# A two-layer decoder step on one core: small norm steps moved to GpSimd, one head's state made later, more room for prefetched caches

## The chip, the cores and the metric

The kernel runs on one NeuronCore of a Trainium2 chip. The metric is the device time of one execution in microseconds (us), less is better. The engines are named as the profile names them: PE (TensorE matmul), PEld (its weight load), DVE (VectorE), ACT (ScalarE), POOL (GpSimd) and SP (SyncE, which issues nearly all DMAs). SBUF is the on-chip memory, PSUM the memory that PE writes.

## The reference, cut to what matters

One inference step of two layers, for a prompt of 256 tokens and 8 samples of one token each, which share all weights. D is 1024. Every layer adds three things to x: a mixer, a cross attention to a memory of 256 rows, and a conv FFN, each on rmsnorm(x). Layer 0 mixes by retention, layer 1 by a gated linear recurrence (LRU).

```python
def rmsnorm(x, g):
    return x * lax.rsqrt(jnp.mean(x * x, axis=-1, keepdims=True) + EPS) * g

def retention_mixer(h, s0, offset, w_in, w_out):
    q, k, v, g = jnp.split(h @ w_in, [nqk, 2 * nqk, 2 * nqk + nv], axis=-1)   # 4 heads
    q, k = rotary(q), rotary(k) * RET_DK ** -0.5
    o, s = retention_scan(q, k, v, s0)          # s: new state, 256 x 512 a head
    o = o * lax.rsqrt(jnp.mean(o * o, axis=-1, keepdims=True) + EPS)          # per head
    return (silu(g) * o) @ w_out, s

def rglru_mixer(...):          # two projections, a conv of width 4, two gates, a scan, an output projection
def cross_attn(h, mk, mv, w_q, w_o):   # softmax(q mk') mv, per head; the samples have caches of their own
def conv_ffn(h, buf, w_up, ...):       # gelu(conv(u)) * g, then w_down
```

All arithmetic is float32. The outputs are y, the new retention, LRU and conv states, and the memory's keys and values.

## The kernel before, in words

**Tiling.** Activations lie with features on the 128 partitions and 264 columns (256 prompt tokens, 8 samples). Each weight matrix comes as chunks of 128x1024 float32 (512 KB), streamed by SP into 6 buffers `wraw`. A chunk is split into a rounded high part `wh` (ACT, line 328, at times DVE, line 460) and the rest `wl` (DVE, line 288). The activations are split into A (or B) in the same way, and each product is three matmuls: wh by high, wh by low, wl by high (`mm3`). Small products (attention in the retention part, sums by a matrix of ones, head states, the LRU's gates) are plain float32 matmuls instead.

**Order of the work.** `run` goes through a list of units (weight chunks with their matmuls) and of plain calls. Between matmuls, a scheduler that runs when the program is built lets other work in: generators (tasks) that issue a few instructions and yield. It decides by a model of each engine's clock (`Clock.op` with a cost per instruction) and by table `POLICY`. What it has decided is fixed: every engine runs its own list in order, and waits by semaphores. So a matmul that is placed too early for its input makes PE wait, and all matmuls behind it.

**Stages.** Retention (all four heads, with the memory's keys and values of layer 0 between), cross attention 0, FFN 0, LRU, cross attention 1, FFN 1, final norm. `enter(nb, ...)` opens a stage: it makes B with `nb` rows of 264 columns, an arena `ar` of what is left of SBUF for temporaries and prefetched tensors, and for `nb` under 24 a second arena of FR = 3072 words. In cross attention that arena (`farena`) holds the split parts of K, q, V and p of `xa_prompt`. `prefetch` loads wanted tensors (sample states, caches) while at most `maxpre` are held and the arena keeps `reserve` words free.

**Norms.** `rsqrt_mean` sums squares over partitions by matmuls with a column of ones (three columns of sums for 264 tokens), makes `a = mean + eps` on DVE, and calls `newton` (line 700): a bit trick for a first guess, then three Newton steps of three small DVE instructions each (128x3 elements). Then PE transposes the result back to rows (`tr`, line 284), ACT copies it to SBUF as `r`. This form is used eight times: for the mixer's norm of x (`g` in `start`), for the memory (`mem_norm(0)`, 128x2 elements), for the heads 0 to 3 (`ret_norm`) and for the norms ahead of both cross attentions (`norm_later`). The norms ahead of FFN and LRU use a wide form.

**A head's new prompt state.** At the end of `ret_attn(h)`, kd (decayed keys, 512 words a partition) and vt (values, 1024 words) are multiplied: 4 float32 matmuls of 512 columns in two PSUM banks, each bank copied by ACT to SBUF and stored to `ret_p`.

**LRU and its end.** The output projection waits at two places for the elementwise chain of each half: `lru_half(1)` before the first three chunks, `lru_half(2)` before the next.

Of the kernel before, what the change touches and what calls it, by code (L numbers as in the profile page):

```python
# [19 lines left out]
P = 128  # L20
# [226 lines left out]
class Kern:  # L247
# [452 lines left out]
    def newton(self, a, y, n, root=False):  # L700

        t = self.get(n)
        tv = t.ap[:, :n]
        if root:
            self.act(y, a, AF.Sqrt)
            self.recip(y, y)
        else:
            self.ts(y.bitcast(I32), a.bitcast(I32), 1, None, ALU.logical_shift_right)
            self.ts(y.bitcast(I32), y.bitcast(I32), -1.0, float(0x5F3759DF), MUL, ADD)
        for _ in range(1 if root else 3):  # L710
            self.tt(tv, y, y, MUL)
            self.stt(tv, a, -0.5, tv, MUL, MUL)
            self.stt(y, tv, 1.5, y, ADD, MUL)
        t.free()

    def rsqrt_mean(self, sq, n, cnt, wide=False, tok=None, root=False):

        b = yield from self.wbank()
        if wide:
            ps = self.ps[:, b, :n]  # L720
            self.mm(ps, self.ones, sq, True, True, False)
            a = self.get(n)
            r = self.get(n)
# [12 lines left out]
        self.unbank(b)  # L736
        self.newton(a.ap[:, :w], a.ap[:, 4:4 + w], w, root)
# [20 lines left out]
    def norm_later(self, wide=False):  # L758
# [3 lines left out]
        def g():  # L762
# [3 lines left out]
            self.r = yield from self.rsqrt_mean(self.sq, NT, float(D), wide)  # L766
# [109 lines left out]
    def retention(self):  # L876
        qkv, gs = [], []
        self.hd = [dict(flags=set()) for _ in range(H)]
        for h in range(H):
            hd = self.hd[h]  # L880

            def ev_rot(b, dt, which, hd=hd, h=h):
# [10 lines left out]
                cs = self.cst[:, C_COS:C_COS + 2 * NT].rearrange("p (a b) -> p a b", a=2)  # L893
                sc = self.cst[:, C_SIN:C_SIN + 2 * NT].rearrange("p (a b) -> p a b", a=2)
# [55 lines left out]
    def ret_qk(self, h):  # L950
# [28 lines left out]
        for jt in range(2):  # L979
            self.act(kd.v(2, 256)[:, jt, :], ps[:, jt * 256:(jt + 1) * 256], AF.Identity,  # L980
                     scale=self.cst[:, C_DEC + 2 * h + jt:C_DEC + 2 * h + jt + 1])
# [20 lines left out]
    def ret_attn(self, h):  # L1002
# [14 lines left out]
        mk = self.cst[:, C_MASK + T * h:C_MASK + T * (h + 1)]  # L1017
# [34 lines left out]
        kd = hd["kd"].v(2, 256)  # L1052
        for dt in range(2):
            b = yield from self.wbank()
            for jt in range(2):
                self.mm(self.ps[:, b, :], kd[:, jt, dt * P:(dt + 1) * P], vv[:, jt, :], jt == 0, jt == 1, False)
            yield WAIT
            so = yield from self.wget(512)
            self.cp(so.ap[:, :512], self.ps[:, b, :])
            self.unbank(b)  # L1060
            self.later_free(lambda so=so, dt=dt: self.store(self.o["ret_p"][h, dt], so.ap[:, :512]), so)
        vt.free()
        hd["kd"].free()
        self.unlock("p")
# [93 lines left out]
    def ret_norm(self, h):  # L1158
# [12 lines left out]
        r = yield from self.rsqrt_mean(s[:, 0, :], NT, 512.0)  # L1171
# [585 lines left out]

POLICY = (
# [6 lines left out]
def tile_hybrid_step(ctx: ExitStack, tc: tile.TileContext, ins, outs):  # L1765
# [10 lines left out]
    K.cst = pool.tile([P, NCST], F32, name="cst")  # L1776
    K.par = pool.tile([P, NPRM], F32, name="par")
    K.qk = ctx.enter_context(tc.tile_pool(name="rows", bufs=1, space=bass.MemoryType.DRAM)).tile([H, 2, S, 256], F32, name="qk")
    K.junkt = pool.tile([P, 2, 256], BF16, name="junkt")
# [22 lines left out]
    FR = 3072  # L1802
    ROOM = 29184 + 1024 * (6 - K.NR) - 128 - 128 - S - 2 * 2 * KD * M

    def enter(nb, maxpre, reserve, slots, main):
        def go():
# [3 lines left out]
            fr = FR if nb < 24 else 0  # L1810
            extra = ROOM - 2 * nb * NT - fr
# [3 lines left out]
            if nb == 16:  # L1815
                K.mn = (bt[:, 0, 8:, :M], bt[:, 1, 8:, :M])
            ar = Arena(pb.tile([P, extra], F32, name=f"x{K.uid}"), extra)
            K.ar = ar
            if fr:
                lend(nb == 16)  # L1820
# [7 lines left out]
    def lend(states):  # L1828
# [8 lines left out]
        box.append((fs, ar))  # L1837

    def unlend():
        fs, ar = box.pop()  # L1840
# [3 lines left out]
    def relend():  # L1844
        unlend()
        lend(False)
# [17 lines left out]
    def leave():  # L1864
        K.drain()
        if len(box[-1]) == 2:
            unlend()
# [5 lines left out]
    def start():  # L1873
# [6 lines left out]
        K.load(K.cst[:, :C_MASK], ins["cst"][:, :C_MASK])  # L1880
# [6 lines left out]
        K.load(K.cst[:, C_MASK:], ins["cst"][:, C_MASK:])  # L1887
# [8 lines left out]
        def g():  # L1896
# [11 lines left out]
            cs = K.cst[:, C_COS:C_COS + 3 * NT].rearrange("p (a b) -> p a b", a=3)  # L1908
# [168 lines left out]
```

## Time and profile before

| what | us |
|---|---|
| median of 3 runs | 1028.97 (1027.68 to 1030.23) |
| the profiled execution, its time | 1026.02 |
| the profiled execution, its span | 1024.2 |
| PE busy | 999.7 (98%) |
| DVE busy | 801.8 (78%) |
| ACT busy | 573.1 (56%) |
| POOL busy | 84.1 (8%) |

A span reaches from the first to the last instruction. The granted clock of PE is 0.996 over the span. Rows of groups read: line of the kernel, engine, operation, output <- input, shape, count, busy time, mean length in ns, idle time before. A row of a timeline reads: start, length of the merged instructions from the first start to the last end, engine, line, operation. Instructions of one engine overlap in the record, since the next starts before the one before has drained: the distance from start to start is what an instruction costs its engine. A float32 matmul of the plain form stands as two records for each instruction of the program (the row that says 512 columns x4 is two instructions).

### The profile page before, as it was taken

The page shows a single profiled execution, that of the slowest core. Times are in us where ns is not written, and L with a number is a line of the kernel's source. Part 1 is how long each engine was busy: PE and PEld are TensorE (multiplying, and loading weights), DVE is VectorE, ACT ScalarE, POOL GpSimd, SP SyncE. Part 2 cuts the span into 40 slices and gives each one's busy share as a digit, 9 for nine tenths or more (in the row PEclk, how much of TensorE's full clock was granted, in tenths as well). Part 3 has the DMA queues.
Part 4 walks back from the last instruction along what each step waited for, and adds up shares of the span by engine and source line. Part 5 has one row for each costly group of instructions (what it writes and reads, how often), then busy time and mean ns, then how long its engine had stood idle before and what let it go on. Part 6 is the DMA issues. An engine that isn't in the chain of part 4 may idle for free.

```text
span 1024.2 us, 20780 instructions
## 1 busy us (share of the span) xinstructions
PE 999.7 (98%) x8042; PEld 949.3 (93%) x8042; DVE 801.8 (78%) x1683; ACT 573.1 (56%) x960; POOL 84.1 (8%) x190
## 2 busy tenths in 40 slices
PE   7999999999999999999999999999999999999996
PEld 7989999899998779999999999989867999999996
DVE  6957888687887635899899777989754998999674
ACT  5544445454555545566666554697444676666552
POOL 0000000000000000122231000300000132221000
PEclk9999999999999999999999999999999999999998
DMA  9568787886677976767798887448876678788961
GB/s 369 196 229 298 270 290 244 324 292 219 225 260 258 340 285 233 223 208 231 279 333 301 297 287 249 154 160 302 296 249 208 224 233 272 279 304 270 332 207 75
DMA packets 75619, 263.89 MB, mean 258 GB/s; under 512 B 8640, under 2 KB 9344, under 8 KB 75008
## 3 DMA queue, kind: packets, MB, share of 16 engines
q1 hardware_dynamic: 75088, 261.98, 73.8%
q8 instruction: 63, 1.03, 0.4%
q10 hardware_dynamic: 432, 0.58, 0.2%
q14 instruction: 36, 0.29, 0.1%
HBM read 237.72 MB, written 24.81 MB: 256 GB/s over the span
## 4 chain that ended last, share of the span: by engine, by line
PE 57%; DVE 4%; DMA 3%; ACT 3%; issue 1%; SPq 0%; DVEq 0%; ACTq 0%
PE ps L269 54%; PE ps L274 2%; ACT x L324 1%; DVE wl L288 1%; DVE x L288 1%; DVE x L294 1%; DMA x<-in_cache_v 1%; ACT L324 1%; DMA x<-in_cache_k 1%; DMA kvt<-in_cache_v 1%; PE ps L284 1%; DMA kvt<-in_cache_k 1%; DMA wraw<-in_lru_w_in 0%; DVE x L313 0%; ACT wh L328 0%
## 5 line engine op out<-in xcount | busy, mean ns | idle before, releaser
L269 PE MATMUL ps<-A,wh 128*128 128x264 f32 x2816 | 524.3, 287 | 7.9 <-ACT A L324 6.6
L269 PEld LDWEIGHTS ps<-A,wh 128*128 128x128 f32 x2816 | 437.7, 189 | 16.0 <-issue 7.0
L328 ACT CAST wh<-wraw 128x1024 fp32r<-128x1024 f32 x283 | 296.2, 1050 | 274.1 <-PE ps L269 211.0
L288 DVE TENSOR_TENSOR wl<-wraw,wh 128x1024 fp32r<-128x1024 f32 x296 | 359.2, 1221 | 80.1 <-ACT wh L328 70.8
L269 PE MATMUL ps<-A,wl 128*128 128x264 f32 x1408 | 400.4, 284 | 0.1
L269 PE MATMUL ps<-B,wh 128*128 128x264 f32 (+1 forms) x1664 | 308.6, 286 | 0.9 <-DVE B L288 0.9
L269 PEld LDWEIGHTS ps<-A,wl 128*128 128x128 f32 x1408 | 265.3, 188 | 0.6 <-DVE wl L288 0.5
L269 PEld LDWEIGHTS ps<-B,wh 128*128 128x128 f32 x1664 | 257.0, 188 | 9.0 <-issue 7.5
L269 PE MATMUL ps<-B,wl 128*128 128x264 f32 (+1 forms) x832 | 235.7, 283 | 1.2 <-DVE wl L288 1.2
L269 PEld LDWEIGHTS ps<-B,wl 128*128 128x128 f32 x832 | 156.3, 188 | 1.4 <-DVE wl L288 1.4
L288 DVE TENSOR_TENSOR x<-ps,x 128x264 f32<-128x264 f32 (+2 forms) x248 | 83.4, 364 | 27.8 <-PE ps L269 18.2
L332 POOL COPY x<-x 128x16 f32<-128x16 f32 (+2 forms) x162 | 77.8, 514 | 257.8 <-DVE x L288 199.0
L324 ACT ACTIVATE x<-x 128x264 f32<-128x264 f32 (+4 forms) x166 | 59.6, 389 | 30.5 <-DVE x L294 17.8
L294 DVE SCALAR_TENSOR_TENSOR x<-x,par 128x280 f32<-128x280 f32 (+3 forms) x128 | 61.7, 488 | 2.3
L294 DVE SCALAR_TENSOR_TENSOR junkt<-f,x 128x256 bf16<-128x256 f32 x104 | 37.8, 421 | 20.9 <-DMA f<-in_state_ret 14.8
L294 DVE SCALAR_TENSOR_TENSOR kvt<-x,vst,kvt 128x256 f32<-128x256 f32 x128 | 53.3, 478 | 0.0
L328 ACT CAST B<-x 128x264 fp32r<-128x264 f32 (+2 forms) x84 | 34.7, 418 | 32.6 <-DVE x L288 25.0
L288 DVE TENSOR_TENSOR x<-x 128x264 f32<-128x264 f32 (+6 forms) x106 | 44.8, 435 | 5.7 <-ACT x L324 3.9
L288 DVE TENSOR_TENSOR B<-x,B 128x264 fp32r<-128x264 f32 (+2 forms) x84 | 36.8, 439 | 8.8 <-ACT B L328 8.6
L324 ACT ACTIVATE x<-x,par 128x280 f32<-128x280 f32 (+2 forms) x64 | 38.6, 605 | 5.1 <-DVE x L288 4.7
L269 PE MATMUL ps<-wh,B 128*128 128x512 f32 x128 | 41.4, 397 | 0.0
L328 ACT COPY x<-ps 128x264 f32<-128x264 f32 (+4 forms) x64 | 22.6, 381 | 32.7 <-PE ps L269 20.4
(90 smaller groups left out, 669.9 us busy)
## 6 DMA issues: line engine op xcount, KB each, us to landing
wraw<-in_ffn_w_up SPq DMA_DIRECT2D x96, 512.0 KB, 4.4
wraw<-in_ret_w_in SPq DMA_DIRECT2D x48, 512.0 KB, 4.8
wraw<-in_ffn_w_down SPq DMA_DIRECT2D x48, 512.0 KB, 5.4
kvt<-in_state_ret SPq DMA_DIRECT2D x38, 512.0 KB, 7.0
out_ret_s<-kvt SPq DMA_DIRECT2D x32, 512.0 KB, 6.0
f<-in_state_ret SPq DMA_DIRECT2D x26, 512.0 KB, 5.3
x<-in_cache_v SPq DMA_DIRECT2D x21, 512.0 KB, 7.1
wraw<-in_xa_w_k SPq DMA_DIRECT2D x16, 512.0 KB, 4.4
```

The source lines that it names most:

```text
L269: self.last = self.nc.tensor.matmul(out, lhsT, rhs, start=start, stop=stop)
L274: self.nc.tensor.matmul(out, lhsT, rhs, start=start, stop=stop, tile_position=(0, LO * j))
L284: self.nc.tensor.transpose(out, in_, self.ident[:n, :n])
L288: self.nc.vector.tensor_tensor(out=out, in0=a, in1=b, op=op)
L294: self.nc.vector.scalar_tensor_tensor(out, a, s, b, op0, op1, **kw)
L324: self.nc.scalar.activation(out, in_, func, **kw)
L328: self.nc.scalar.copy(out, in_)
L332: self.nc.gpsimd.tensor_copy(out, in_)
```

## The change

- **Newton steps on POOL.** `newton` has a flag `aside`. With it the three steps run as four `nc.gpsimd` instructions each (12 in all) instead of three on DVE (9 in all); the scheduler's model books 130 ns for each. Set for the norm of x, the memory's norm and the heads 0, 1 and 2. Head 3 and the norms of `norm_later` keep DVE.
- **Head 2's state later.** In `ret_attn(2)` kd and vt are stored to a DRAM tensor `sv` (parked). In the LRU part `state_back(2)` loads them back (768 KB), and `state_gen` makes the state with 8 float32 matmuls of 256 columns. `fill(2, n)` issues n of them at three places: 3 after `lru_half(1)`, 3 after `lru_half(2)`, 2 before cross attention 1. The other heads also use 8 matmuls of 256 columns.
- **Room.** Only the identity and the ones (256 columns of the constants) stay in SBUF for the whole program. The rotary tables, decays and masks (1824 words a partition) lie in a tile `tab` of the first stage. The later stages' arenas grow by that. In the LRU and cross attention 1 stage the second arena shrinks from 3072 to 2048 words, and `maxpre` goes from 3 to 5.

```diff
-    def newton(self, a, y, n, root=False):
+    def newton(self, a, y, n, root=False, aside=False):
...
         for _ in range(1 if root else 3):
+            if aside:
+                for out, ins in ((tv, (y,)), (tv, (tv, a)), (tv, (tv,)), (y, (y, tv))):
+                    self.c.op("pool", 130.0, [out], list(ins))
+                self.nc.gpsimd.tensor_tensor(out=tv, in0=y, in1=y, op=MUL)
+                self.nc.gpsimd.tensor_tensor(out=tv, in0=tv, in1=a, op=MUL)
+                self.nc.gpsimd.tensor_scalar(tv, tv, -0.5, 1.5, MUL, ADD)
+                self.nc.gpsimd.tensor_tensor(out=y, in0=y, in1=tv, op=MUL)
+                continue
             self.tt(tv, y, y, MUL)
...
-    def rsqrt_mean(self, sq, n, cnt, wide=False, tok=None, root=False):
+    def rsqrt_mean(self, sq, n, cnt, wide=False, tok=None, root=False, aside=True):
...
+        if h in PARKED:
+            self.later_free(lambda: self.store(self.sv[h][:, :512], hd["kd"].ap[:, :512]), hd["kd"])
+            self.later_free(lambda: self.store(self.sv[h][:, 512:], vt.ap[:, :1024]), vt)
+        else:
+            for dt in range(2):
+                b = yield from self.wbank()
+                for half in range(2):
+                    for jt in range(2):
+                        self.state_mm(b, hd["kd"], vt, dt, half, jt)
+                yield WAIT
+                yield from self.state_out(b, h, dt)
...
+    def state_mm(self, b, kd, vt, dt, half, jt):
+        c = slice(half * 256, (half + 1) * 256)
+        self.mm(self.ps[:, b, c], kd.v(2, 256)[:, jt, dt * P:(dt + 1) * P], vt.v(2, 512)[:, jt, c], jt == 0, jt == 1, False)
...
+    def fill(self, h, n):
+        def go():
+            for _ in range(n):
+                next(self.fills[h], None)
+        return go
...
-        r = yield from self.rsqrt_mean(s[:, 0, :], NT, 512.0)
+        r = yield from self.rsqrt_mean(s[:, 0, :], NT, 512.0, aside=h < H - 1)
...
+PARKED = (2,)
...
-    K.cst = pool.tile([P, NCST], F32, name="cst")
+    K.cst = pool.tile([P, C_COS], F32, name="cst")
...
+            fr = {16: 3072, 8: 2048, 24: 0}[nb]
+            extra = ROOM - 2 * nb * NT - fr - (TAB if nb == 16 else 0)
...
-    items += [policy(3), enter(8, 3, 4500, (), 6), lambda: K.want_cache(1)] + K.lru()
+    items += [policy(3), enter(8, 5, 4500, (), 6), K.state_back(2), lambda: K.want_cache(1)] + K.lru()
...
-    items += out(w, [K.lru_half(1), pairs(w, (0, 1, 2), (0,)), K.lru_half(2), tune(12, 3500, (0,), 6),
+    items += out(w, [K.lru_half(1), K.fill(2, 3), pairs(w, (0, 1, 2), (0,)), K.lru_half(2), K.fill(2, 3), tune(12, 3500, (0,), 6),
...
-    items += [policy(4), tune(14, 3500, (0,), 4, 1)] + K.xattn(1)
+    items += [policy(4), tune(14, 3500, (0,), 4, 1)] + [K.fill(2, 2)] + K.xattn(1)
```

Since the scheduler's clock sees other costs and sizes, the order of much of the work shifts. Three places matter below. The first is DVE at the norm of head 0's output, in the kernel before. `x_85` is the stage's arena, `junkt` the thrown-away product of the samples' dot products with the old states (`f_89`), `cst` the constants.

```order
L288 TENSOR_TENSOR wl<-wraw,wh 128x1024
L301 TENSOR_SCALAR x_85<-ps 128x3
L299 TENSOR_SCALAR x_85<-x_85 128x3
L301 TENSOR_SCALAR x_85<-x_85 128x3
L288 TENSOR_TENSOR x_85<-x_85 128x3
L294 SCALAR_TENSOR_TENSOR x_85<-x_85 128x3 x2
```

After two more such steps DVE goes on with other work. In the changed kernel DVE has, at the same norm, this (`x_89` is the arena, `f_93` the states):

```order
L301 TENSOR_SCALAR x_89<-ps 128x3
L299 TENSOR_SCALAR x_89<-x_89 128x3
L301 TENSOR_SCALAR x_89<-x_89 128x3
L288 TENSOR_TENSOR wl<-wraw,wh 128x1024
L294 SCALAR_TENSOR_TENSOR junkt,x_89<-f_93,x_89 128x256 x12
L288 TENSOR_TENSOR wl<-wraw,wh 128x1024
L288 TENSOR_TENSOR x_89<-x_89 128x528 x2
```

The Newton steps are gone from DVE, and the instructions that stood behind them follow the three guesses at once. The second place is POOL, which before has nothing between its start and the four `vst` products of the retention part. In the changed kernel its list begins so (one Newton step of the first norm; eight more rows like the last four end that norm):

```order
L714 ISA
L714 TENSOR_TENSOR x_89<-x_89 128x3
L715 TENSOR_TENSOR x_89<-x_89 128x3
L716 TENSOR_SCALAR x_89<-x_89 128x3
L717 TENSOR_TENSOR x_89<-x_89 128x3
```

Five norms put 60 such instructions there, each waiting for the one before. The third place is PE at the two ends of head 2's state. Before, at the end of its attention (`x_85` holds kd and vt):

```order
L269 MATMUL ps<-x_85 128x512 x2
L269 MATMUL ps<-A,wh 128x264 x2
L269 MATMUL ps<-A,wl 128x264
L269 MATMUL ps<-x_85 128x512 x2
L269 MATMUL ps<-A,wh 128x264 x2
```

In the changed kernel these are absent there, and at `lru_half(1)` PE has (`x_6722` is the LRU stage's arena, `B_6721` the projection's input):

```order
L269 MATMUL ps<-A,wl 128x264
L269 MATMUL ps<-x_6722 128x256 x3
L269 MATMUL ps<-B_6721,wh 128x264 x2
L269 MATMUL ps<-B_6721,wl 128x264
L269 MATMUL ps<-B_6721,wh 128x264 x2
```

The same three stand again within the B rows at `lru_half(2)`, and two stand before the first A row of cross attention 1.

## Rows read from the trace of the kernel before

**Rows 1.** The page, part 1: busy time and share of the span by engine.

```profile
PE 999.7 (98%) x8042; PEld 949.3 (93%) x8042; DVE 801.8 (78%) x1683; ACT 573.1 (56%) x960; POOL 84.1 (8%) x190
```

**Rows 2.** Windows: stretch, its length, then busy time (instructions) by engine, clock, DMA.

```profile
20.00:300.00 280.00, 278.83 (x2107) 264.06 (x2105) 222.66 (x597) 137.27 (x221) 2.18 (x5) 1.00 0.76 264
...
440.00:460.00 20.00, 20.00 (x168) 20.00 (x167) 19.28 (x53) 12.74 (x22) 4.09 (x12) 1.00 0.61 201
...
640.00:725.00 85.00, 81.76 (x613) 78.28 (x612) 77.68 (x143) 62.23 (x94) 11.12 (x24) 1.00 0.62 217
725.00:805.00 80.00, 76.04 (x705) 62.12 (x704) 50.58 (x106) 39.20 (x94) 0.00 (x0) 1.00 0.68 233
```

**Rows 3.** Waits of PE in the LRU and cross attention 1: total us, times, longest.

```profile
PE ps L269 <- DVE wl L288: 1.2, 1, 1.2
...
PE ps L269 <- DVE B L288: 0.9, 1, 0.9
...
PE ps L274 <- DMA x<-in_cache_v: 1.6, 1, 1.6
PE ps L274 <- DMA kvt<-in_cache_v: 0.9, 2, 0.5
...
PE ps L274 <- DMA kvt<-in_cache_k: 0.4, 1, 0.4
```

**Rows 4.** Timeline of PE at the end of head 2's attention.

```profile
125.43 1.88 PE L269 MATMUL ps<-x 128*128 128x512 f32 x4
...
129.47 0.28 PE L269 MATMUL ps<-A,wl 128*128 128x264 f32 x1
```

**Rows 5.** Timeline of PE at the first norm: sums, next matmul, transposes.

```profile
20.46 0.72 PE L269 MATMUL ps<-cst,sq 128*128 128x1 f32 x6
21.05 0.49 PE L269 MATMUL ps<-A,wh 128*128 128x264 f32 x2
...
24.42 0.49 PE L284 MATMUL ps<-cst,x 128*128 128x128 f32 x3
```

**Rows 6.** Timeline of DVE at the first norm: mean, first Newton instruction, last two.

```profile
21.23 0.16 DVE L301 TENSOR_SCALAR x<-ps 128x3 f32<-128x3 f32 x1 [2.31 <-PE ps L269]
...
21.83 0.16 DVE L288 TENSOR_TENSOR x<-x 128x3 f32<-128x3 f32 x1
...
23.20 0.36 DVE L294 SCALAR_TENSOR_TENSOR x<-x 128x3 f32<-128x3 f32 x2
```

**Rows 7.** Timelines of POOL and of DVE beside it, in FFN 0.

```profile
427.80 2.33 POOL L332 COPY x<-x 128x2 f32<-128x2 f32 x2 [2.31 <-DVE x L288]
...
427.72 2.35 DVE L288 TENSOR_TENSOR wl<-wraw,wh 128x1024 fp32r<-128x1024 f32 x2
...
447.84 0.34 POOL L332 COPY x<-x 128x2 f32<-128x2 f32 x2 [5.45 <-DVE x L288]
...
447.36 0.83 DVE L288 TENSOR_TENSOR x<-ps,x 128x256 f32<-128x256 f32 x3
```

**Rows 8.** Groups of POOL by shape, whole span.

```profile
L332 POOL COPY x<-x 128x3 f32<-128x3 f32 x8 | 5.4, 672 | 17.6 <-DVE x L288 17.5
...
L1033 POOL TENSOR_TENSOR vst<-x 128x32 f32<-128x32 f32 x3 | 1.0, 327 | 114.2 <-ACT x L328 83.8 <-DVE junkt L294 30.4
```

**Rows 9.** Timeline of DVE behind head 0's norm: one split, dot products with states.

```profile
107.92 1.22 DVE L288 TENSOR_TENSOR wl<-wraw,wh 128x1024 fp32r<-128x1024 f32 x1
109.05 0.42 DVE L294 SCALAR_TENSOR_TENSOR junkt<-f,x 128x256 bf16<-128x256 f32 x1
...
109.40 0.42 DVE L294 SCALAR_TENSOR_TENSOR junkt<-f,x 128x256 bf16<-128x256 f32 x1
```

**Rows 10.** Groups of DVE by shape, whole span.

```profile
L460 DVE CAST wh<-wraw 128x1024 fp32r<-128x1024 f32 x13 | 9.0, 691 | 9.9 <-PE ps L269 9.8
...
L288 DVE TENSOR_TENSOR f<-kvt,f 128x512 fp32r<-128x512 f32 x16 | 10.9, 684 | 0.5 <-ACT f L328 0.5
```

**Rows 11.** Timeline of PE at the sums of head 1's norm.

```profile
140.32 0.80 PE L269 MATMUL ps<-cst,x 128*128 128x1 f32 x6 [0.35 <-DVE x L288]
```

More of the change, by code (lines that the diff above doesn't have):

```diff
@@ L765, in g @@
             yield self.c.written(self.sq)
-            self.r = yield from self.rsqrt_mean(self.sq, NT, float(D), wide)
+            self.r = yield from self.rsqrt_mean(self.sq, NT, float(D), wide, aside=False)
         def go():
@@ L1051, in ret_attn @@
         hd["flags"].add("attn")
-        kd = hd["kd"].v(2, 256)
-        for dt in range(2):
[L1054 to L1061, printed above, removed]
@@ L1062, in ret_attn @@
-        vt.free()
-        hd["kd"].free()
-        self.unlock("p")
+        if h in PARKED:
[9 more added lines that the diff above has]
+                yield from self.state_out(b, h, dt)
+            vt.free()
+            hd["kd"].free()
@@ new lines, in ret_attn, with state_out, state_back, g @@
+        self.unlock("p")
+    def state_mm(self, b, kd, vt, dt, half, jt):
+        c = slice(half * 256, (half + 1) * 256)
+        self.mm(self.ps[:, b, c], kd.v(2, 256)[:, jt, dt * P:(dt + 1) * P], vt.v(2, 512)[:, jt, c], jt == 0, jt == 1, False)
+    def state_out(self, b, h, dt):
+        so = yield from self.wget(512)
+        self.cp(so.ap[:, :512], self.ps[:, b, :])
+        self.unbank(b)
+        self.later_free(lambda: self.store(self.o["ret_p"][h, dt], so.ap[:, :512]), so)
+    def state_back(self, h):
+        def go():
+            def g():
+                b = yield from self.wget(1536)
+                self.load(b.ap[:, :1536], self.sv[h])
+                self.back[h] = b
+            self.add(g(), 0)
+            self.fills[h] = self.state_gen(h)
+        return go
@@ new lines, in state_gen @@
+    def state_gen(self, h):
+        self.until(lambda: h in self.back)
+        buf = self.back[h]
+        kd, vt = (Buf(buf.ap[:, o:], None, 0, 0) for o in (0, 512))
+        for dt in range(2):
+            self.until(lambda: self.aux)
+            b = min(self.aux, key=self.bank_at)
+            self.aux.remove(b)
+            for half in range(2):
+                for jt in range(2):
+                    self.state_mm(b, kd, vt, dt, half, jt)
+                    if half * jt:
+                        self.add(self.state_out(b, h, dt), 1, self.c.t["pe"])
+                        if dt:
+                            buf.free()
+                    yield
@@ L1066, in later_free, with go @@
+    def fill(self, h, n):
+        def go():
+            for _ in range(n):
+                next(self.fills[h], None)
+        return go
     def later_free(self, fn, buf):
@@ L1775, in tile_hybrid_step @@
     K.locks = {}
-    K.cst = pool.tile([P, NCST], F32, name="cst")
+    K.cst = pool.tile([P, C_COS], F32, name="cst")
     K.par = pool.tile([P, NPRM], F32, name="par")
     K.qk = ctx.enter_context(tc.tile_pool(name="rows", bufs=1, space=bass.MemoryType.DRAM)).tile([H, 2, S, 256], F32, name="qk")
+    K.sv = ctx.enter_context(tc.tile_pool(name="parked", bufs=1, space=bass.MemoryType.DRAM)).tile([H, P, 1536], F32, name="sv")
+    K.back, K.fills = {}, {}
     K.junkt = pool.tile([P, 2, 256], BF16, name="junkt")
@@ L1819, in go @@
             if fr:
-                lend(nb == 16)
+                lend(nb == 16, fr)
             tune(maxpre, reserve, slots, main)()
@@ L1826, in enter, with lend @@
         return go
-    def lend(states):
+    def lend(states, FR):
         fs = ExitStack()
@@ L1836, in lend @@
             K.farena = ar
-        box.append((fs, ar))
+        box.append((fs, ar, FR, 0))
     def unlend():
-        fs, ar = box.pop()
+        fs, ar, FR, _ = box.pop()
         K.until(lambda: ar.holes == [(0, FR)])
@@ L1845, in relend @@
         unlend()
-        lend(False)
+        lend(False, 3072)
     def tune(maxpre, reserve, slots, main, p=2):
@@ L1865, in leave @@
         K.drain()
-        if len(box[-1]) == 2:
+        if len(box[-1]) == 4:
             unlend()
@@ L1879, in start @@
         K.fetch()
-        K.load(K.cst[:, :C_MASK], ins["cst"][:, :C_MASK])
+        K.load(K.cst, ins["cst"][:, :C_COS])
+        K.load(K.tab[:, :3 * NT], ins["cst"][:, C_COS:C_MASK])
         def split():
@@ L1886, in start @@
         split()
-        K.load(K.cst[:, C_MASK:], ins["cst"][:, C_MASK:])
+        K.load(K.tab[:, 3 * NT:], ins["cst"][:, C_MASK:])
         K.load(K.par[:, NG:], ins["par"][:, NG:])
```

19 lines of the change are left out of this document (9 added, 10 removed).

## The prediction

> **What bounds the kernel now.** I read the page's busy times first: PE is busy for 98% of the span, DVE for 78% [rows 1]. A busy PE need not be at its peak, so I read the windows next. In a steady stretch PE takes 168 matmuls in 20 us, 0.119 us each [rows 2]; that is the pace of nearly all its work. In the retention part, 20 to 300 us, it is idle for only 280 - 278.83 = 1.2 us, in the LRU for 85 - 81.76 = 3.2 us, in cross attention 1 for 80 - 76.04 = 4.0 us [rows 2]. The change gives PE the same work (four matmuls of 512 columns become eight of 256). So it can win only the idle time in those windows, and it loses whatever new wait it puts ahead of PE's list. The waits say what the idle time is: in the LRU PE waits 1.2 us for a low weight part at its first output matmuls and 0.9 us for B's low part before the second half; in cross attention 1 it waits 1.6 + 0.9 + 0.4 = 2.9 us for caches [rows 3].
>
> **Head 2's state.** From the first state matmul to the last row shown lie 129.47 - 125.43 = 4.04 us, with five ordinary matmuls inside [rows 4]: 4.04 - 5 x 0.119 = 3.44 us for four of 512 columns, 0.86 us each, so 0.43 us for one of 256. Retention loses 3.4 us of PE work, in a stretch where PE has almost no idle time. The LRU part gets 8 x 0.43 = 3.4 us. The first three (1.29 us) stand right before the matmuls that wait 1.2 us, the next three before those that wait 0.9 us: 2.1 us vanish in waits, 1.3 us are new work. Net -2.1. Ends: 0 if the waits lie elsewhere after the reordering, -3.4 if the last pair meets a wait too. The parking adds two stores of 768 KB together and a load of as much; at the retention's 264 GB/s and a DMA share of 0.76 [rows 2] that is 2.9 us of queue time. I cost it at 0, since weights come chunks ahead, and up to +2.9 if that cover is gone. SP issues three more DMAs, and one more for the constants that are loaded in two pieces; behind them wait weight chunks that are not needed at once: 0.
>
> **Room for caches.** Loads of caches move ahead of the weight stream in SP's list, by two to four loads of 512 KB. What is late is the stream itself, so I take half of the 2.9 us: -1.5, ends 0 and -2.9. The second arena loses its third place: the split of V must then wait until the scores have read K and q. The nearest row is that split's DVE half, 0.68 us [rows 10], once a head; ends 0 and 4 x 0.68 = +2.7. I take +0.3, as PE hardly waits for softmax until the last head.
>
> **Newton steps, the deciding term.** Before, the nine DVE instructions take 23.20 + 0.36 - 21.83 = 1.73 us [rows 6]. Five norms go: 45 instructions leave DVE, 60 come to POOL. DVE's relief is worth little, as PE waits for DVE's sums once for 0.35 us at head 1 [rows 11]: -0.3, ends 0 and -0.4. The price is the delay of the result, for which PE waits in order at the transposes.
>
> How long may POOL take? At the first norm the sums are through at 21.05 [rows 5] and DVE begins Newton at 21.83 [rows 6], 0.78 us later. In the changed order 39 matmuls stand between sums and transposes at the first norm (27 before), 36 at head 0, 39 at head 2, and at head 1 15 matmuls with four float32 ones of 256 and four of 128 columns. At 0.119 us, 0.43 and 0.22 us that is 4.6, 4.3, 4.6 and 4.4 us; less 0.78, POOL has 3.8, 3.5, 3.8 and 3.6 us. The memory's norm has 27 matmuls, four float32 ones and eight transposes (0.1 us each, from three that last 0.49 us with their drain [rows 5]), 3.2 + 1.3 + 0.8 - 0.8 = 4.5 us net.
>
> How long will it take? The trace has no such chain. Undisturbed, two small POOL copies take 0.34 us together, beside DVE instructions that read PSUM [rows 7], and one product of 32 columns 0.33 us at the mean [rows 8]. I take 0.25 us: 12 x 0.25 = 3.0 us, no wait anywhere. But beside DVE instructions that read two tensors in SBUF, POOL stands still: at 427.80 two such copies take 2.33 us, as long as the two weight splits beside them, 2.35 us [rows 7], and the eight copies of 3 columns average 0.67 us [rows 8]. One POOL instruction gets through for each such DVE instruction. And that is what the changed order puts behind the three guesses: at heads 0 and 2 a weight split (1.13 us from start to start) and twelve dot products of 0.35 us [rows 9]. Twelve POOL steps then need 1.13 + 11 x 0.35 = 5.0 us, 1.5 us too long at head 0 and 1.2 us at head 2. At head 1: a cast of 0.69 us [rows 10], eight dot products, a split, two more products, 0.69 + 10 x 0.35 + 1.13 = 5.3 us, 1.7 us too long. At the first norm: split, cast, split, then DVE itself waits for the result, so 3 steps in 2.95 us and 9 free ones in 2.25, 1.4 us too long. At the memory's norm: three steps beside PSUM readers, two in a cast and a split, 0.75 + 1.8 + 7 x 0.25 = 4.3 us, no wait. Sum 5.8 us if DVE never pauses. It is busy 222.66 of 280 us there [rows 2], 80%: +4.6. Ends: 0 (free steps) and twice the DVE instructions for each step, about 5 us a norm at four norms, +20; the nearest row has one for one, so I stay near it.
>
> The cast is the weak piece of this: no row shows POOL beside a DVE cast, and I count it like the split because it reads SBUF as well. If it does not hold POOL, the first norm and head 1 each get about 0.4 us back and the term falls to some 3.9 us. The Trainium skill, "GPSIMD Engine Reference", section Specifications, speaks for holding: it says that POOL shares its SBUF interface with VectorE and contends with instructions that have two SBUF inputs (427.80 agrees) or that run in a mode with two ports, which a cast as fast as this one (128x1024 in 0.69 us) may do. By that the sum stays at +4.6; by the rows alone it lies between 3.9 and 4.6.
>
> **Sum.** -2.1 - 1.5 + 0.3 - 0.3 + 4.6 = +1.0 us on the profiled execution of 1026.02 us (span 1024.2 and 1.8 us around it), 1027.0. The median of the runs lies 2.95 us above that execution, so about 1030.0 as a median. A measurement of this kernel can tell about 0.3%, 3.1 us, from no change.
>
> **Rivals.**
>
> *POOL runs free.* DVE pauses for states' loads, or POOL slips in; the chain takes 3 us and PE never waits. For it: PE's transposes were moved 12 matmuls later at the first norm. Against it: DVE is busy 80% there. Then -2.1 - 1.5 + 0.3 - 0.3 = -3.6: 1025.4.
>
> *POOL is starved.* Each step misses the gap between two DVE instructions, or meets weight splits of 1.13 us. Without Newton the sum is -3.6, so the kernel is slower by over 3.1 us once Newton costs more than 6.7 us, 1.7 us of waiting at each of four norms. With two dot products of 0.35 us a step, twelve steps take 8.4 us, 4.7 us longer than the 3.7 they may take at the mean of the four norms: 4 x 4.7 x 0.8 = 15 us in all. The middle of 6.7 and 15 is 10.9: +7.3, 1036.3. For it: each step waits for the one before, so it may always arrive when the next DVE instruction has begun. Against it: at 427.80 the alternation is one for one.
>
> *The change doesn't do what it says.* The reordering moves the two LRU waits away from the fills (chunks split at other times), and cache loads are as late as before: 0 and 0 instead of -3.6, with the Newton term: +4.6, 1033.6. For it: the wait for the low weight part hangs on DVE's list, which changes.
>
> **How the numbers follow.** Forecast 0.45 (1026 to 1033 by itself), POOL free 0.27, starved 0.17, no effect 0.11. Faster by over 0.3% (below 1025.9) is the free case's better part and a little of the forecast: 0.25. Slower by over 0.3% (above 1032.1): the starved case, most of the last and a little of the forecast, 0.30. The rest, 0.45, is within. Of the free case I leave out what lies below 1023.5 (all caches won and no wait at all), of the starved one what lies above 1037: range 1023.5 to 1037.
>
> **What would show it.** POOL rows of 128x3 between 20 and 200 us: a mean near 0.4 us (twelve in about 5 us) for the forecast, near 0.2 for free, 0.6 and more for starved. PE waits at line 284 for POOL at four transposes, 1 to 2 us each. At the first B matmuls the float32 rows of 256 columns stand where PE waited, and the waits for the low weight part and for B are gone. The waits at line 274 for caches fall to half. I am wrong if PE has no wait for POOL, or one over 3 us, or if the retention part has new waits for weights or states that none of this names.

## The result, and the profile after

| | median of the runs, us | ratio to before (95% interval) |
|---|---|---|
| before, 6 runs | 1029.45 (1025.24 to 1033.42) | |
| changed, 6 runs | 1024.79 (1022.17 to 1026.13) | 0.9948 (0.9923 to 0.9973) |
| changed, 12 further runs (before beside them 1028.85) | 1025.70 (1023.70 to 1027.38) | 0.9963 (0.9947 to 0.9979) |

The change makes the kernel 0.4 to 0.5% faster, 3 to 5 us. I had forecast +1.0 us for the profiled execution and 1030.0 us for the median, no measurable change.

The page of the changed kernel, busy time by engine, against [rows 1]:

```profile
PE 996.5 (98%) x8074; PEld 953.7 (93%) x8074; DVE 797.7 (78%) x1639; ACT 572.8 (56%) x959; POOL 104.8 (10%) x250
```

The span is 1022.0 us, 2.2 less than before. A second profiled execution of the changed kernel has a span of 1024.6 us, so spans alone would not show the gain. Of the 76 timed runs of the kernel before, only 6 were faster than its profiled execution (1026.02 us): the profile of before is a fast one, and the medians are the better measure of the whole. The profiles serve to find the stages.

PE's idle time rose from 1024.2 - 999.7 = 24.5 to 1022.0 - 996.5 = 25.5 us. That this is 1.0 us, the sum that I had forecast for the time, is chance. PE's busy time fell by 3.2 us, with the same work (the 32 further records are the state matmuls in halves). So some of what stood in the record as busy was waiting. To see where, take windows of each kernel from the sums of one norm to those of the next. First before, then changed: retention, cross attention 0, LRU, cross attention 1 (the dots stand for FFN 0). Columns are stretch, length, busy time (instructions) of PE, PEld, DVE, ACT, POOL, clock, DMA share and GB/s.

```profile
20.46:290.64 270.18, 269.51 (x2032) 254.95 (x2030) 214.82 (x571) 131.50 (x210) 2.18 (x5) 1.00 0.76 262
290.64:421.22 130.58, 129.08 (x1074) 111.96 (x1072) 82.63 (x157) 66.61 (x137) 0.11 (x1) 1.00 0.76 264
...
632.68:720.25 87.57, 84.33 (x632) 80.78 (x631) 80.98 (x146) 62.08 (x93) 11.53 (x27) 1.00 0.62 217
720.25:808.12 87.87, 83.91 (x770) 69.95 (x769) 56.91 (x124) 43.43 (x101) 0.00 (x0) 1.00 0.69 236
```

```profile
19.53:292.50 272.97, 267.04 (x2048) 258.09 (x2046) 209.44 (x526) 131.24 (x208) 22.71 (x65) 1.00 0.78 268
292.50:423.73 131.23, 128.95 (x1074) 111.79 (x1073) 82.62 (x157) 66.69 (x137) 0.10 (x1) 1.00 0.71 250
...
635.21:722.20 86.99, 85.98 (x637) 82.28 (x636) 81.00 (x146) 63.10 (x95) 11.54 (x27) 1.00 0.67 238
722.20:805.74 83.54, 82.39 (x783) 70.62 (x781) 57.84 (x125) 42.40 (x100) 0.00 (x0) 1.00 0.72 244
```

Retention is 2.8 us longer, cross attention 0 0.65 longer (within its scatter, below), LRU 0.6 and cross attention 1 4.3 us shorter, though the last two took head 2's eight matmuls in. FFN 0 (211.5 us) and FFN 1 (205.4) are the same in both. One more difference needs care: the first sums stand at 19.53 instead of 20.46 us. In kernels with the same order up to there they stand at 19.5 to 21.1 us, so that is scatter.

The waits of PE in the changed kernel (us, times, longest), against [rows 3, 11]:

```profile
PE ps L284 <- POOL x L717: 4.1, 5, 1.4
PE ps L269 <- DVE x L288: 2.5, 2, 1.5
...
PE ps L274 <- DMA x<-in_cache_v: 1.7, 3, 0.9
```

The waits for the low weight part and for B's low part are gone, as forecast. The transposes wait for POOL at five norms, 4.1 us. In the whole kernel the list's waits for caches fall from 3.4 to 1.7 us, in cross attention 1 alone from 2.9 to 0.4 us (to 3.3 and 1.3 us in the second profiled execution). That does not explain 4.3 us in this one stage.

**Where the waiting hid.** The samples' matmuls of line 274 last 0.385 us in the record but follow each other in about 0.06 us: twelve of them last 1.06 us, (1.06 - 0.39) / 11 = 0.061. Before, at the places where PE waits for a cache in cross attention 1 (timeline; in square brackets what the profile counts as idle):

```profile
750.57 0.63 PE L274 MATMUL ps<-x 128*32 128x256 f32 x4
752.84 1.06 PE L274 MATMUL ps<-x 128*32 128x256 f32 x12 [1.65 <-DMA x<-in_cache_v]
...
764.91 0.63 PE L274 MATMUL ps<-kvt,x 128*32 128x256 f32 x4
765.90 1.06 PE L274 MATMUL ps<-kvt,x 128*32 128x256 f32 x12 [0.37 <-DMA kvt<-in_cache_k]
...
777.24 0.63 PE L274 MATMUL ps<-kvt,x 128*32 128x256 f32 x4
778.35 1.06 PE L274 MATMUL ps<-kvt,x 128*32 128x256 f32 x12 [0.49 <-DMA kvt<-in_cache_v]
780.24 0.44 PE L284 MATMUL ps<-cst,x 128*128 128x128 f32 x2 [0.83 <-ACT x L328]
780.61 0.63 PE L274 MATMUL ps<-kvt,x 128*32 128x256 f32 x4
781.65 1.06 PE L274 MATMUL ps<-kvt,x 128*32 128x256 f32 x12 [0.41 <-DMA kvt<-in_cache_v]
```

Four matmuls need 4 x 0.061 = 0.24 us, but the twelve after them begin 2.27, 0.99, 1.11 and 1.04 us after the first of the four: waits of 2.03, 0.75, 0.87 and 0.80 us, 4.4 us together, where the brackets say 2.9. The transposes at 780.24 come 1.89 us after twelve that need 0.73: 1.16 us for a bracket of 0.83. So these five places cost 5.6 us, not 3.75. In the changed kernel only the first has a successor:

```profile
750.86 0.62 PE L274 MATMUL ps<-x 128*32 128x256 f32 x4
751.92 1.06 PE L274 MATMUL ps<-x 128*32 128x256 f32 x12 [0.43 <-DMA x<-in_cache_v]
```

The same count over all matmuls of line 274 that follow another in cross attention 1 (start to start, less 0.061 us each) gives 8.0 us in the kernel before and 3.3 in the changed one.

**What the limit does.** The LRU stage begins at 632.68 us before and at 635.21 after. SP's issues of the fourth and fifth cache load from there on, before and then changed:

```profile
700.36 0.43 SPq L345 DMA_DIRECT2D kvt<-in_cache_k  x1
700.84 0.43 SPq L345 DMA_DIRECT2D x<-in_cache_k  x1
```

```profile
658.00 0.42 SPq L345 DMA_DIRECT2D kvt<-in_cache_k  x1
...
662.06 0.43 SPq L345 DMA_DIRECT2D x<-in_cache_k  x1
```

Before, they go out 68 us into the stage, with the limit of 5 loads 23 and 27 us into it, and the loads behind them move up by two places.

**The fills.** The wait for the low weight part before, and what stands there after:

```profile
689.12 0.40 PE L269 MATMUL ps<-B,wh 128*128 128x264 f32 x2
690.76 0.39 PE L269 MATMUL ps<-B,wl 128*128 128x264 f32 x1 [1.23 <-DVE wl L288]
```

```profile
691.58 1.46 PE L269 MATMUL ps<-x 128*128 128x256 f32 x6
692.68 0.59 PE L269 MATMUL ps<-B,wh 128*128 128x264 f32 x2
693.21 0.39 PE L269 MATMUL ps<-B,wl 128*128 128x264 f32 x1
```

Three fills (six records) and the first B matmuls follow without a gap in the record.

**POOL's chain.** Timeline of POOL and then of DVE at the first norm after; the remaining rows of POOL read like the fourth. Against [rows 6]:

```profile
20.94 1.10 POOL L714 TENSOR_TENSOR x<-x 128x3 f32<-128x3 f32 x1 [20.50 <-DVE x L301]
22.12 0.53 POOL L715 TENSOR_TENSOR x<-x 128x3 f32<-128x3 f32 x1
22.73 1.25 POOL L716 TENSOR_SCALAR x<-x 128x3 f32<-128x3 f32 x1
24.07 0.19 POOL L717 TENSOR_TENSOR x<-x 128x3 f32<-128x3 f32 x1
...
26.27 0.19 POOL L717 TENSOR_TENSOR x<-x 128x3 f32<-128x3 f32 x1
```

```profile
20.77 1.22 DVE L288 TENSOR_TENSOR wl<-wraw,wh 128x1024 fp32r<-128x1024 f32 x1
21.91 0.69 DVE L460 CAST wh<-wraw 128x1024 fp32r<-128x1024 f32 x1
22.70 1.23 DVE L288 TENSOR_TENSOR wl<-wraw,wh 128x1024 fp32r<-128x1024 f32 x1
```

Each of the first three steps ends where DVE's instruction beside it ends: split, cast, split. Then nine free ones at 0.27 us. At the heads, DVE was not always at such instructions. At head 1 it paused for 1.44 us ahead of its cast, and five of POOL's twelve steps went free meanwhile:

```profile
126.03 0.69 DVE L460 CAST wh<-wraw 128x1024 fp32r<-128x1024 f32 x1 [1.44 <-PE ps L269]
```

From first start to last end the five chains take 5.5 us (first norm), 4.7 (memory), 4.6, 4.1 and 4.7 (heads 0, 1, 2). PE's transposes wait until 26.52, and again for rotary at 30.71:

```profile
26.52 0.54 PE L284 MATMUL ps<-cst,x 128*128 128x128 f32 x3 [1.43 <-POOL x L717]
...
30.71 0.48 PE L269 MATMUL ps<-A,wh 128*128 128x264 f32 x2 [1.48 <-DVE x L288]
```

### The profile page after: what moved, and what is told of

It is laid out like the page before. It is cut to its first block, busy times and chain, and to the rows that moved or that the text cites. A ratio compares the mean times of both kernels' runs of the same rounds, so it can differ in the third digit from the quotient of the medians.

```text
span 1022.0 us, 20880 instructions
## 1 busy us (share of the span) xinstructions
PE 996.5 (98%) x8074; PEld 953.7 (93%) x8074; DVE 797.7 (78%) x1639; ACT 572.8 (56%) x959; POOL 104.8 (10%) x250
## 4 chain that ended last, share of the span: by engine, by line
PE 84%; DVE 5%; DMA 4%; issue 2%; ACT 2%; POOL 2%; SPq 0%; DVEq 0%; ACTq 0%; POOLq 0%
PE ps L269 81%; PE ps L274 2%; DMA x<-in_cache_v 2%; DVE wl L288 1%; PE ps L284 1%; DVE x L294 1%; DVE x L288 1%; ACT x L324 1%; ACT wh L328 1%; DMA f<-in_state_ret 1%; POOL x L714 1%; POOL x L716 0%; DMA wraw<-in_lru_w_in 0%; POOL x L717 0%; POOL x L715 0%
## 5 line engine op out<-in xcount | busy, mean ns | idle before, releaser
L324 ACT ACTIVATE x<-x 128x264 f32<-128x264 f32 (+3 forms) x162 | 58.0, 388 | 22.4 <-DVE x L288 10.1
L288 DVE TENSOR_TENSOR x<-x 128x264 f32<-128x264 f32 (+4 forms) x87 | 40.8, 482 | 7.5 <-ACT x L324 6.1
```

Of the source, the lines that this page charges most:

```text
L288: self.nc.vector.tensor_tensor(out=out, in0=a, in1=b, op=op)
L324: self.nc.scalar.activation(out, in_, func, **kw)
```

## Experiments

A stage's length is read as above. From one profiled execution to the next it varies by about 1 us in the stages that wait for loads: the second one of the changed kernel has retention 272.32, cross attention 0 132.27, LRU 88.19, cross attention 1 84.56. "Before" beside a median is the kernel before, timed together with that run. Its medians lie between 1027.63 and 1029.45, so medians that were not timed together compare to 1 or 2 us.

### Newton back on DVE, same order

```diff
-                self.nc.gpsimd.tensor_tensor(out=tv, in0=y, in1=y, op=MUL)
+                self.nc.vector.tensor_tensor(out=tv, in0=y, in1=y, op=MUL)
...
```

> The changed kernel with its twelve Newton steps on DVE in place of POOL, at the same place in the program; the scheduler's bookkeeping is left alone, so PE, ACT and SP keep their lists word for word. Theory A (POOL's stall is a real price of 4.1 us at the five transposes, and the gain comes from elsewhere): twelve DVE steps of about 0.19 us take 2.3 us, all five POOL waits at line 284 go, PE idle in 20 to 300 us falls from 5.9 to about 1.5 us; the time falls by 4 to 5.6 us, to about 1019.5. Rival B (the relief of DVE is where the gain came from): the split behind each norm comes 2.3 us later, PE waits for low weight parts instead, 5 x 1 to 2 us, the time rises by 1 to 5 us, to 1026 to 1030.

Measured: 1019.84 us, before 1027.63, ratio 0.992 (0.9902 to 0.9938). The changed kernel stood at 0.9948 and 0.9963. Its retention window:

```profile
20.34:289.54 269.20, 266.48 (x2048) 258.02 (x2046) 218.23 (x586) 131.62 (x208) 4.89 (x5) 1.00 0.78 271
```

Theory A holds: 269.2 against 273.1 at the mean of the four profiles of this order with POOL (272.97, 272.32, 273.40, 273.85), so POOL's price is 3.9 us. B is out.

### No state move

```diff
-PARKED = (2,)
+PARKED = ()
...
-    items += [policy(3), enter(8, 5, 4500, (), 6), K.state_back(2), lambda: K.want_cache(1)] + K.lru()
+    items += [policy(3), enter(8, 5, 4500, (), 6), lambda: K.want_cache(1)] + K.lru()
...
-    items += [policy(4), tune(14, 3500, (0,), 4, 1)] + [K.fill(2, 2)] + K.xattn(1)
+    items += [policy(4), tune(14, 3500, (0,), 4, 1)] + K.xattn(1)
```

> The changed kernel with no head parked: head 2's state is made in its own attention again, nothing is stored to and loaded from the parking tensor, the three fills are gone; POOL's Newton steps and the room for caches stay. Theory A (the move is worth the two LRU waits that it fills, as forecast 2.1 us): slower than the changed kernel by about 2 us; waits of 1.2 and 0.9 us for the low weight part and for B are back at the first and the third group of output chunks. Rival B (the move is the main source of the gain): slower by 4 us or more. Rival C (the waits only moved): within 1 us.

Measured: 1029.98 us, before 1027.63, ratio 1.0018 (1.0004 to 1.0033): 4 to 5 us slower than the changed kernel, so B's number. But it does not sit where either theory had it. The LRU's two waits are back, 1.2 and 0.9 us, as A said; yet LRU and cross attention 1 are 87.21 and 84.24 us, as long without the fills as the changed kernel's with them. The loss is in retention:

```profile
20.57:297.95 277.38, 270.32 (x2063) 261.18 (x2062) 210.68 (x528) 130.14 (x208) 22.31 (x65) 1.00 0.75 261
```

277.4 against 273.1, 4.3 us: 3.3 of PE busy time (270.32 to the changed kernel's 267.04), which are the matmuls, and about 1 us of idle time. With Newton on DVE the same step is worth less (next but one).

### The LRU stage's room undone, and half of that

```diff
-            fr = {16: 3072, 8: 2048, 24: 0}[nb]
+            fr = {16: 3072, 8: 3072, 24: 0}[nb]
...
-    items += [policy(3), enter(8, 5, 4500, (), 6), ...
+    items += [policy(3), enter(8, 3, 4500, (), 6), ...
```

> The changed kernel with the LRU stage's second arena at 3072 words and its limit of loads ahead at 3 again, as before; everything up to the LRU is the same. Theory A (the waits for caches were far larger than the 2.9 us that the list of waits showed, since each of the 256 sample matmuls of cross attention 1 costs 0.063 us but stands in the record for 0.385 us, so that the record of one covers the first 0.3 us of the wait of the next; from start to start these 256 take 22.4 us before and 16.8 us after): slower than the changed kernel by 4 to 5.6 us. Rival B (the list of waits is right and half of it was won): slower by 1 to 1.5 us. Rival C (the smaller second arena cost as much as the caches gave): within 0.5 us.

With the second line alone:

> The changed kernel with the LRU stage's limit of loads ahead at 3 again, and the second arena left at 2048 words. Theory A (the limit is what held the caches back): cross attention 1 takes 87 to 88 us as it does with both undone, the time rises by 3 to 4 us. Rival B (the 1024 words that the arena gains are what let one more cache in): cross attention 1 stays near 83.5 us and the time within 1 us of the changed kernel's.

Measured: 1027.84 us (before 1027.63, ratio 0.9997, 0.9985 to 1.0008), and 1028.44 us (before 1028.85, ratio 0.9991, 0.9975 to 1.0007), where the changed kernel, timed together with the latter, took 1025.70. Their cross attention 1:

```profile
721.96:809.84 87.88, 83.88 (x782) 70.71 (x781) 57.24 (x124) 43.32 (x101) 0.00 (x0) 1.00 0.72 244
```

```profile
724.25:812.79 88.54, 83.66 (x782) 70.93 (x781) 57.61 (x125) 42.57 (x100) 0.00 (x0) 1.00 0.71 243
```

Both are back at before's 87.87, 3.3 to 5.0 us above the changed kernel's two profiles (83.54 and 84.56), and the matmuls of line 274 lose 6.1 and 6.6 us from start to start again. With the limit of 3 the fourth and fifth cache load go out 68 us into the LRU stage again. So it is theory A, though the medians say 2.1 to 3.7 us, less than A's 4 to 5.6 for the first run. Without the limit of 5 loads ahead the gain is gone; the 1024 words of the second arena add nothing that shows. Whether the limit would do it without the words that the constants leave free no run here tests.

### Room only

Newton on DVE as before, no parked head; the loading back and the fills are gone as above.

```diff
-            if aside:
+            if False:
...
-PARKED = (2,)
+PARKED = ()
```

> The changed kernel with all Newton steps on DVE as before (the scheduler books them there) and no head parked: of the change only the room for caches is left, and the heads' states as 8 matmuls of 256 columns for 4 of 512. Theory A (the caches are the gain): 3.5 to 5 us below the kernel before, 1024.5 to 1026; the 256 sample matmuls of cross attention 1 take 17 to 18 us. Rival B (caches as forecast): 1.2 us below the kernel before, within what can be told from nothing; the 256 sample matmuls take over 20 us. Under both the waits of 1.2 and 0.9 us in the LRU stay.

Measured: 1021.78 us, before 1027.63, ratio 0.9937 (0.9919 to 0.9956): the room alone gains 5.9 us by medians, more than the whole change and a little more than A said. Retention and cross attention 1:

```profile
20.38:290.56 270.18, 269.37 (x2063) 261.06 (x2062) 214.51 (x571) 131.65 (x210) 2.65 (x5) 1.00 0.74 262
719.35:803.39 84.04, 81.81 (x770) 69.78 (x769) 57.19 (x124) 43.43 (x101) 0.00 (x0) 1.00 0.67 237
```

Retention is before's, cross attention 1 is 3.8 us shorter. Against the kernel with the move and Newton on DVE: 270.18 to 269.20, 1.0 us for the 3.4 us of matmuls that leave; in the medians 1021.78 to 1019.84. PE's busy time there falls by 2.9 us (269.37 to 266.48), but its idle time rises from 0.8 to 2.7 us. The kernel with the move keeps the order that was made for POOL, with its waits (1.1 us for rotary behind the first norm among them), and this one has an order made for DVE. So this pair compares two orders as well.

### Only Newton on POOL, in the kernel before

```diff
+            if aside:
...
+                self.nc.gpsimd.tensor_tensor(out=tv, in0=y, in1=y, op=MUL)
...
-        r = yield from self.rsqrt_mean(s[:, 0, :], NT, 512.0)
+        r = yield from self.rsqrt_mean(s[:, 0, :], NT, 512.0, aside=h < H - 1)
```

> The kernel before with nothing changed but the Newton steps of the same five norms on POOL. The LRU and cross attention 1 stay as before. Theory A (POOL's price adds up from the same terms, the waits at the transposes and the wait behind the first norm): 4 to 8 us slower than before; in the kernel with no parked head the retention part took 277.4 us with POOL and 270.2 us without, 7.2 us. Rival B (the price comes only with the changed order of the other parts): within 2 us of before.

Measured: 1033.71 us, before 1028.85, ratio 1.0044 (1.0026 to 1.0062): 4.9 us slower, theory A. All of it and more is in retention, 277.82 against 270.18, 7.6 us; cross attention 1 stays at 88.3:

```profile
20.05:297.87 277.82, 270.23 (x2031) 255.04 (x2030) 210.62 (x528) 130.23 (x208) 22.20 (x65) 1.00 0.75 260
```

### Two Newton steps on POOL

```diff
-        for _ in range(1 if root else 3):
+        for i in range(1 if root else 3):
             if aside:
                 ...
+                if i == 2: continue
                 self.nc.gpsimd.tensor_tensor(out=tv, in0=y, in1=y, op=MUL)
```

> The changed kernel with two Newton steps on POOL in place of three (8 instructions a norm for 12; the third step is left out), all other work in the same order. Theory A (the length of the chain on POOL is the price): beside dot products a chain gets 1.4 us shorter, where it is free 1.1 us; of PE's waits for POOL (1.6, 0.75, 1.2, 0.6 and 0.8 us from start to start) only about 0.5 us at the first norm is left, and the 1.6 us behind the first norm falls as much; 5 us faster than the changed kernel, about 1020. Rival B (the waits have another cause: the sums come late, or the hand-over to POOL and back costs a fixed time): the waits stay and the time falls by less than 1.5 us.

Measured: 1021.29 us, before 1028.24, ratio 0.9932 (0.9911 to 0.9953). Its waits and its retention part:

```profile
PE ps L269 <- DVE x L288: 2.8, 3, 1.5
...
PE ps L284 <- POOL x L718: 0.3, 1, 0.3
```

```profile
19.77:288.17 268.40, 266.11 (x2048) 258.05 (x2046) 209.18 (x526) 131.44 (x208) 16.88 (x45) 1.00 0.78 271
```

Theory A in the main: with four steps fewer a norm, PE's waits for POOL fall from 4.1 to 0.3 us, retention from 273.1 to 268.4. By medians it is 3.5 to 4.4 us, a little under A's 5. One part of A was wrong: the wait for rotary behind the first norm stays at 1.5 us. It does not hang on the length of POOL's chain; with Newton on DVE in the same order 0.85 to 1.1 us of it are left.

### The first norm alone on DVE, the nine-step form, and a new order

```diff
             if aside:
+                if self.r0 is None:
+                    self.nc.vector.tensor_tensor(out=tv, in0=y, in1=y, op=MUL)
+                    self.nc.vector.scalar_tensor_tensor(out=tv, in0=a, scalar=-0.5, in1=tv, op0=MUL, op1=MUL)
+                    self.nc.vector.scalar_tensor_tensor(out=y, in0=tv, scalar=1.5, in1=y, op0=ADD, op1=MUL)
+                    continue
```

> The changed kernel with the Newton steps of the first norm alone on DVE, in nine instructions; the other four norms stay on POOL, all other work in the same order. Theory A (each norm pays for itself, and the 1.6 us that PE waits a little behind the first norm belongs to that norm's lateness): the waits of 1.6 and 1.6 us become one of about 1.0 us as in the kernel with all steps on DVE, the others stay; 2.2 us faster than the changed kernel. Rival B (the second wait has nothing to do with POOL): 1.6 us faster. Rival C (what one norm gains the next gives back, since DVE and not POOL is what is late): within 0.7 us.

Measured: 1023.47 us, before 1028.24, ratio 0.9948 (0.9929 to 0.9966); retention 270.70, 2.4 us below 273.1. A fits the stage, while the medians (1.3 and 2.2 us below the changed kernel's two) can't tell A from B.

The same three lines for all five norms:

> The changed kernel with its five norms' Newton steps on DVE in the old form of nine instructions a norm (five multiplied and added in pairs), at the same place, and all other work in the same order. Fifteen DVE instructions of about 0.19 us fewer than with twelve a norm: 0.6 us sooner a norm. Theory A (what is left of PE's waits in the retention part hangs on DVE's list): 1 to 2 us below 1019.8, at 1018 to 1019. Rival B (DVE's length there is covered): within 0.7 us of 1019.8.

Measured: 1020.23 us, before 1028.85, ratio 0.9912 (0.9884 to 0.9941); retention 268.98. B: DVE's length is covered there.

Newton on DVE by the old code, with the scheduler told so (`if aside:` becomes `if False:`):

> The changed kernel with the Newton steps of all norms on DVE, and the scheduler told so: it books them on DVE and puts the transposes and the work between in other places. Theory A (the order was made for POOL's long chain, 36 to 39 matmuls between sums and transposes, and with a chain of 2 us on DVE it is already free of waits): no gain over the same order with DVE, 1019 to 1021. Rival B (the order around the norms costs the 4.4 us by which the retention part still exceeds its matmuls): 2 us better, near 1018.

Measured: 1024.97 us, before 1028.24, ratio 0.9965 (0.995 to 0.998). Neither theory: 5 us slower than the same instructions in the old order, retention 272.66 and cross attention 0 133.28. No norm waits any more, but PE now waits for B's split late in retention and runs slowly behind it (last section). The best versions are those that keep the changed kernel's order and have Newton on DVE, with twelve or nine instructions: both beat both kernels, by 0.8 to 0.9% against before.

## Why the prediction was wrong

**The step that failed is the room for caches**, "What is late is the stream itself, so I take half of the 2.9 us: -1.5, ends 0 and -2.9". With the +0.3 for the second arena that made -1.2. Measured: cross attention 1 takes 87.9 us in the kernel before, 88.3 with Newton alone, 87.9 and 88.5 with the limit back, and 83.1 to 84.6 in all others. Between the first two profiles that is 4.3 us, by the second profile of the changed kernel 3.3, both outside the ends that I had given. By medians the room is worth 2.7 us (limit back, timed together with the changed kernel) to 5.9 us (room alone). Two things were wrong in the step.

- The size of the wait. I took the list's 2.9 us [rows 3]. It counts from the end of a record that outlasts its matmul's cost by 0.3 us. From start to start the same waits are 4.4 us, and 1.2 us more in the transposes among them.
- The half. I argued as if the stream were full. But in the LRU part the DMA engines were busy for a share of 0.62 [rows 2], and what was late was the issue: two cache loads that the limit of 3 kept until 68 us into the stage went out after 23 and 27 us. The share rose to 0.67 (0.64 with the limit back, where only the parked state comes in), and weights were not late for it.

With 4.3 for 1.2 the sum is +1.0 - 3.1 = -2.1, and the first two spans differ by 2.2. That they agree is luck: what else I missed cancels (retention 1.9 us worse than the sum has it, the LRU 1.1 better, the rest scatter), and the second span of the changed kernel is 0.4 us above that of before.

**Head 2's state: the work and the LRU's waits were right, the price of the fills was not.** I had retention at -3.4 and the LRU and cross attention 1 at +1.3, -2.1 in sum. PE's busy time in retention does fall by 2.9 to 3.3 us, and the LRU's two waits stand in the four profiles without fills and in none of the nine with them. But the LRU and cross attention 1 cost nothing: with the fills in, LRU takes 86.5 to 88.2 us, without them 87.2 to 87.6. And retention wins 4.3 us where Newton is on POOL and only 1.0 where it is on DVE, since PE's idle time falls by about 1 us in the first pair and rises by 1.9 in the second, which compares two orders. By medians the move is worth 1.9 us with Newton on DVE, so that this is near the 2.1 of the forecast is in part luck. The 2.9 us of queue time in the forecast count 768 KB once, though stores and load together are twice that; no wait for them shows in any list.

**Newton on POOL: right in mechanism, near in size by luck.** Forecast +4.6. Measured in retention: 3.9 us against the same order with DVE; 7.2 us between the two kernels with the room and no parked head, and 7.6 when done alone (4.9 by medians). The first norm and heads 0, 1 and 2 wait 1.4, 1.0, 0.4 and 0.7 us, where I had 1.4, 1.5, 1.7 and 1.2 before the factor 0.8. The memory's norm, which I had without a wait, waits 0.6 us. The sum comes near because that wait and the first norm's make up for the heads: there DVE paused for 1.0 to 1.4 us, and POOL's steps went free meanwhile. I had taken a fifth off each wait for such pauses, but a pause shortens the whole chain, of which the wait is only the end. Not in my sum at all are the waits around the norms: 1.5 us for rotary behind the first, and, where head 2's state stays in place, 0.9 and 1.4 us at the sums of head 0.

Beside DVE's splits, casts and dot products the steps go one for one, and the cast holds POOL as the split does (0.53 us at 22.12). That settles the weak piece in the way that the Trainium skill has it: "GPSIMD Engine Reference", section Specifications, names DVE instructions with two SBUF inputs or in a mode with two ports. The trace agrees as far as the cast's 0.53 us; which mode the cast ran in no row here tells.

**DVE's relief: about nothing, as said.** Twelve instructions a norm or nine on DVE make 269.20 and 268.98. The wait for rotary belongs in the main to the transposes' new place, 12 matmuls later in the order: two POOL steps in place of three leave it at 1.5 us, and DVE in the same order at 0.85 to 1.1, while the three kernels with the transposes in the old place and Newton on DVE (before, room only, new order) have none there.

**The rivals.** Free POOL gave 1025.4, near what was measured, but for a false reason: POOL does cost 4 us or more. The starved case and the case without effect are out.

**From the profile to the median** I added 2.95 us, and the medians of before stayed near where that puts them (1027.63 to 1029.45). But the two spans of the changed kernel, 1022.0 and 1024.6, differ by more than the first of them differs from before's; one profiled execution can't carry a forecast to 1 us, and I had left that out of the range's reasoning.

## What to carry to other kernels

Before pricing a wait, compare starts with starts: where records are much longer than the pitch of their instructions, the idle list misses most of a short wait, and a fall in "busy" at equal work is how it shows afterwards. Before calling a stream full, read its DMA share in the stage where the loads would go, and when its issues go out. And a chain of small dependent steps doesn't get cheaper on an idle engine when that engine must stand still beside the busy one: at least 3.9 us were lost here to save DVE time that nothing waited for.

## What the hardware showed that I had not expected

- A cast of 128x1024 on DVE holds a tiny POOL instruction for 0.53 us, one split for 1.10 to 1.25 us; free, the same instruction lasts 0.19 us and the next follows after 0.27 us. DVE doesn't slow down: its splits last 1.22 and 1.23 us beside POOL and 1.22 alone [rows 9].
- In the kernel with Newton on DVE and the new order, PE was idle for 1.53, 0.28 and 0.28 us between 262.3 and 266.3 us, with six matmuls between. Then the granted clock fell to half, the 1.2 GHz level; from 274 us on it is back at 1.00. Ten of this kernel's twelve timed runs have a granted clock of 0.992 to 0.994, where the changed kernel's eighteen have 0.996 or 0.997. The first of the matmuls behind the long wait, and windows of 2 us:

```profile
263.81 0.86 PE L269 MATMUL ps<-B,wh 128*128 128x264 f32 x2 [1.53 <-ACT B L328]
```

```profile
262.00:264.00 2.00, 0.47 (x4) 0.25 (x2) 1.52 (x4) 0.41 (x1) 0.00 (x0) 1.00 0.87 332
264.00:266.00 2.00, 1.56 (x6) 0.78 (x5) 1.35 (x4) 1.40 (x3) 0.00 (x0) 1.00 0.97 270
266.00:268.00 2.00, 1.72 (x5) 1.08 (x4) 1.21 (x4) 0.69 (x2) 0.00 (x0) 0.53 0.94 322
268.00:270.00 2.00, 2.00 (x10) 1.95 (x10) 1.48 (x2) 0.00 (x0) 0.95 (x1) 0.50 0.97 324
```

PE takes ten matmuls in the last 2 us, 0.2 us each, where 0.119 is its pace [rows 2]. The single wait of 2 us at 750.6 in the kernel before did not do that: the clock stays at 1.00 behind it.

```profile
752.00:754.00 2.00, 1.16 (x13) 0.56 (x14) 0.00 (x1) 0.00 (x0) 0.00 (x0) 1.00 0.90 301
```
